# Operand pads, full rows for a filter product, and one wait for two PSUM banks in a hybrid RWKV-7 and Conformer kernel

## The chip, the cores and the metric

The kernel runs on one core of one Trainium2 chip. The metric is the time of one execution on the device in microseconds. A run of this kind gives the same kernel's time within a few tenths of a per cent: the three runs of the kernel before lie between 1447.48 and 1453.27 us, with a median of 1452.06 us. Beside them stands one execution under the hardware profiler, from which all traces here are taken.

## What is computed

A backbone of two layers over 512 latent tokens of 1024 channels, with 256 context tokens as a prefix. Each layer norms its input, scales and shifts it by values made from a conditioning vector, mixes, norms again and adds the result through a gate. All numbers are float32.

```python
def even_mixer(h, hc, ...):            # layer 0
    r, k, v, za, bg, cg, xb, zb = jnp.split(h @ w_in, EVEN_SPLITS, axis=-1)
    # context first: its final states S_f, S_b start the latent scans
    ya, _, _ = rwkv_seq(rwkv_prep(h, r, k, v, *rw), S_f, S_b, r_k, lnx_w, lnx_b, True)
    yb = bg * dwconv(cg * xb, sc_w, seg_len)
    y = jnp.concatenate([ya * silu(za), yb * silu(zb)], axis=-1) @ w_out

def odd_mixer(h, ...):                 # layer 1
    u, gl, z = jnp.split(h @ w_in, 3, axis=-1)        # 1024 -> 3 x 2048
    a = u * jax.nn.sigmoid(gl)
    a = dwconv(a, dw_w, seg_len) + dw_b               # 31 taps in rows of 64 tokens
    a = layer_norm(a, ln_w, ln_b)
    return (silu(a) * silu(z)) @ w_out                # 2048 -> 1024
```

`rwkv_seq` is a recurrence over the tokens, forwards and backwards, with a 64x64 state for each of 16 heads.

## The kernel before, in words

**Dense products.** Every large product is made of float32r matmuls with 128 rows, 128 columns and up to 512 moving elements. To keep float32's precision each operand is split into a high part (cast to float32r) and a low part (what is left), and `mm3` adds three matmuls: high by high, high by low, low by high. `hilo` (lines 119 to 126) loads a weight block, casts it on ScalarE (line 126) and subtracts on VectorE (line 127). All matmuls but the transposes go through line 57, so in the profile they are told apart by their tiles.

**The even layer.** The 16 heads are handled in 8 pairs, the 512 latent tokens in 8 chunks of 64. Within a chunk the recurrence is a triangular system that is solved in one piece, and a short chain passes the state from chunk to chunk. The work comes in 12 stages, 4 for the context (two pairs each) and 8 for the latent tokens (one pair each). In stage s the chain of stage s runs (`chain_lat`: tiles `zol`, `uh`, `UV`, `Hl`, `Ol`), and around it the stages after it are prepared: `solve` (`Xl`, `Yl`, `xtmpl`) and `merge` for s+1, `light` and `heavy` for s+2, and as filling for TensorE the projections and gates (`pl`, `pza`) or a head group of the convolution branch (`conv_branch`: `pcg`, `pxb`, `pbg`, `pzb`).

`heavy` is the part that the change touches. Its function `pa` makes the head products `E` of a pair in four groups (direction z, half g): for two heads h, four products of 64 rows each, written in turn to one PSUM bank for each head (`pal`), then two evictions by VectorE that multiply with a mask (line 601). `pb` transposes the keys of a pair, for each direction 16 transposes in turn into two banks (`pbl`), with two evictions by ScalarE (line 612). Both take their banks from the tag `at`, which has two, and which `light`, `pv`, `po` and others use as well.

**What sets the order.** The kernel is written stage by stage, and a planner that lays out each engine's queue takes, of the instructions that are ready by its own clock, the one written first. It gives the banks of a tag in the order of their first use. `pinned()` (line 561) ties the matmuls of a group to the order in which they are written, but lets other work stand between them. `issue_after` and the `HEAVY_AFTER` table hold a group behind a step of the running chain. On the chip each engine then runs its queue in order, with semaphores between engines.

**The odd layer.** The output product of layer 0 (`o`) and the norm of layer 1 lead to the tiles `h1h` and `h1l`. For each of 4 column blocks n and 4 row blocks m, `products` makes two products `pu` of 24 matmuls each (weights `wc`, in the tags `wa` and `wb`), `gated` joins them and splits the result into `ah`, and the 31-tap convolution is done as a product with a transform of 119 rows (`forward`, tile `px`), a multiplication with the transformed filter, and a product back (`back`, tile `pc`). The tile `ah` holds for each half of 64 tokens the high part in one half of the rows and the low part in the other. `forward` multiplies it with `dfh`, which holds the high part of the transform in both halves (128 rows), and then with `dfl`, the transform's low part, on the 64 rows of the high part alone. Then follow 16 products `pz` of 24 matmuls for z (weights `wz`), and the output product `f` of 384 matmuls (inputs `y`, in the tags `wb` and `xr`; weights `wf`, in the tag `wz`).

**Where tiles lie.** A pool lays its tags one behind the other in SBUF, each rounded up to 32 bytes a partition. In the pool of the odd layer come first `h1h`, `h1l`, `wz`, `a` (all sizes multiples of 64 bytes, starting on one), then `dfc` (960 bytes), `dbe` (32), `dinv` (256), four small ones, and then `pt`, `raw`, `wa` and `wb`: these last ones, `xr` and `pr` start 32 bytes past a multiple of 64. In the even layer the pools of the latent inputs and weights (`hlh`, `hll`, `w`) and of the output product start 32 bytes past one, and so does all that follows the 4-byte tile `ones` up to `xtmp`, the tile `E` among it; `AR`, `BK`, `BKt`, `UV` and `H` start on a multiple.

Of the kernel before, what the change touches and what calls it, by code (L numbers as in the profile page):

```python
# [8 lines left out]
F32 = mybir.dt.float32  # L9
# [42 lines left out]
def kernel(ctx: ExitStack, tc: tile.TileContext, I: dict, out: bass.AP):  # L52
# [14 lines left out]
    def const(name, shape, dt=F32):  # L67
        return cp.tile(shape, dt, tag=name, name=name)

    ident = const("ident", [P, P])  # L70
    epsr = const("epsr", [P, 3])
    G.memset(epsr[:, 0:1], RMS_EPS)
    G.memset(epsr[:, 1:2], LN_EPS)
    G.memset(epsr[:, 2:3], GN_EPS)
    nc.sync.dma_start(ident, I["ident"])

# [90 lines left out]
    def ps_at(name):  # L167
# [8 lines left out]
    SIZE = {"AR": D, "BK": 1536, "BKt": D, "UV": 2 * D, "O": 768, "X": D, "E": 4 * D, "P": 528, "H": 256, "HP": 256,  # L176
            "h0": 256, "PC0": 8, "PC1": 8, "rnq": 48, "xtmp": 136}

# [6 lines left out]
    def small(name, shape):  # L185
        return cvp.tile(shape, F32, tag=name, name=name)

    ones = small("ones", [P, 1])
    G.memset(ones, 1.0)
    omu, hmu, hka, oka = (small(n, [P, k]) for n, k in (("omu", 24), ("hmu", 24), ("hka", 8), ("oka", 8)))  # L190
# [9 lines left out]
    lorl = [[cvp.tile([P, SEQ], F32R, tag=f"{t}{z}", name=f"{t}{z}") for z in range(2)] for t in ("tanhl", "xal")]  # L200
    hlat = tuple(hlp.tile([P, KT, SEQ], F32R, tag=t, name=t) for t in ("hlh", "hll"))
    E0 = w("E", "hctx", F32R).rearrange("p (a k c) -> p a k c", a=2, k=KT)
    hch, hcl = E0[:, 0], E0[:, 1]
# [302 lines left out]
    def lightz(st, z):  # L506
        lat, nm, parts, low, kk = (st[x] for x in ("lat", "nm", "parts", "low", "kk"))
        k_, r_, bon = st["k"], st.get("r"), st.get("bon")
        pl = low(0, z, f"lw{nm}{z}")
        for p, cs in parts:  # L510
            S.activation(sg[:, cs.start // CH : cs.stop // CH, 1:65], ch3(pl[:, cs]), AF.Tanh,
                         bias=hc("w0", z * 8 + p), scale=0.5)
        S.activation(sg[:, :, 1:65], sg[:, :, 1:65], AF.Identity, bias=ones)
        pl = low(1, z, f"la{nm}{z}")
        a = w("a", f"a{nm}{z}")
        for p, cs in parts:
            S.activation(a[:, cs], pl[:, cs], AF.Tanh, bias=hc("a0", z * 8 + p), scale=0.5)
        cumf = w("P", f"P{nm}{z}")
# [41 lines left out]

    def pinned():
        prev = []

        def go(o, lhsT, rhs, start=True, stop=True, op=mm):
            e = op(o, lhsT, rhs, start, stop)
            if prev:
                tc.add_manual_dep(e.ins, prev[-1].name,
                                  mybir.DependencyInfo(mybir.DependencyClass.NoSync, mybir.DependencyReason.DATA),
                                  reason="written order")
            prev[:] = [e.ins]  # L570
            return e

        return go
# [7 lines left out]
    def heavy(st, an=None):  # L581
# [7 lines left out]
        def pa():  # L589
            for gi, (z, g) in enumerate(PA_ORDER if lat else ((0, 0), (1, 0))):  # L590
                with anchored(an, ha[gi if lat else 2 * gi]):
                    AR, BK = st["AR"][z], st["BK"][z]
                    m, x = (4, P) if lat else (8, CH)
                    c0 = m * g
                    pas = [ch3(ps_at(f"pa{nm}{z}{g}{h}"), x) for h in range(2)]
                    go = pinned()
                    for c in range(m):
                        for h in (1, 0):
                            go(pas[h][:, c, :], kb(BK, h, c0 + c), AR[ZR[h], c0 + c, 0:x])
                    for h in range(2):  # L600
                        V.tensor_tensor(out=E[:, h, z * NLAT + c0 : z * NLAT + c0 + m, :], in0=pas[h],  # L601
                                        in1=maskE[:, z * (1 + h) : z * (1 + h) + 1, 0:x].to_broadcast([P, m, x]), op=ALU.mult)

        def pb():
            for z in range(2):
                pbs = [ch3(ps_at(f"pb{nm}{z}{h}")) for h in range(2)]
                go = pinned()
                for c in range(NLAT):
                    for h in (1, 0):
                        go(pbs[h][:, c, :], kb(st["BK"][z], h, c), ident[ZR[h], ZR[h]], op=tr)  # L610
                for h in range(2):
                    S.copy(st["BKt"][z][:, :, ZR[h]], pbs[h])

# [375 lines left out]

    acc0 = outproj(0, ("mm0", "mm1", "at", "at"), ORDER, held, early)  # L990
    l0.close()
    with ExitStack() as l1:
# [71 lines left out]
        dfw = lt("a", "dfw")[:, :NPROD]  # L1064
        dfc = big("dfc", [P, 2 * NPROD + 2], F32R)
        dfh, dfl = dfc[:, :NPROD], dfc[:, NPROD : 2 * NPROD]
        dbe = big("dbe", [P, 8])[:NPROD, 0:1]
        dinv = big("dinv", [NPROD, 64])
# [16 lines left out]
        def dft_stages(n, m, ahl):  # L1085
            pr = [lt("pr", f"pr{n}{m}{s}") for s in range(2)]

            def forward():
# [3 lines left out]
                for s in range(2):  # L1092
                    tp(px[s][:NPROD], dfl[64 * s : 64 * s + 64, :], ahl[s][64 * s : 64 * s + 64, :], False, True)
                for s in range(2):
# [107 lines left out]
        w2 = I["od_w_out"][0]  # L1202
        gg = gate_rows(1)
        xres = [lt("wa", f"xo{m}") for m in range(4)]
        for m in range(4):
# [120 lines left out]
```

## Time and profile before

| | before |
|---|---|
| runs | 1453.27, 1447.48, 1452.06 us |
| median | 1452.06 us |
| the profiled execution | 1451.59 us |
| its span, first to last instruction | 1449.6 us |
| mean granted TensorE clock | 0.979 |

The span is a little shorter than the time of the execution, which has a start and an end around it. In the rows below PE stands for TensorE's matmuls, PEld for its weight loads, DVE for VectorE, ACT for ScalarE, POOL for GpSimd. A row of the timeline gives start, length, engine, line, operation, what is written and read (buffer numbers left out) and how many alike follow each other; matmuls overlap, so their pace is read from start to start, not from their length.

### The profile page before, as it was taken

To read this page: it belongs to the slowest core of one execution; us is meant where nothing else is said; L and a number is where in the kernel's file an instruction comes from. 1 tells how busy PE (TensorE), PEld (TensorE's weight loads), DVE (VectorE), ACT (ScalarE), POOL (GpSimd) and SP (SyncE) were. 2 spreads that over 40 slices of the span, in tenths; PEclk is the share of its full clock that TensorE was granted. 3 is DMA by queue.
4 is the path that set the end of the run, shared out by engine and by line. 5 is a ranking of instruction groups with operands and counts; after the bars stand their busy time and mean duration, and the time that the engine had idled before them with its cause. 6 is when DMAs were issued, how large, how long until landed. Compare 5 with 4: busy or idle time off the path is not lost. (4 is left out here: it accounts for less than half of the span.)

```text
span 1449.6 us, 29729 instructions
## 1 busy us (share of the span) xinstructions
PE 1407.2 (97%) x11921; PEld 1012.7 (70%) x11921; DVE 983.7 (68%) x2294; ACT 749.5 (52%) x1516; POOL 118.2 (8%) x246
## 2 busy tenths in 40 slices
PE   6999999999998999999999999999999999999998
PEld 1564677878776766666676666778777777788876
DVE  2675597568688989999999998557745544544333
ACT  4536364364664665756666565456753323464222
POOL 2023210000101101011011100010000000000000
PEclk9999999979897999999999999999999999999999
DMA  9755433312222321222222212359803303133322
GB/s 324 221 172 160 153 110 98 97 52 71 83 85 74 92 69 59 81 86 60 76 67 83 91 49 84 131 175 324 252 34 102 117 22 95 58 102 91 99 89 86
DMA packets 137626, 158.54 MB, mean 109 GB/s; under 512 B 15375, under 2 KB 104143, under 8 KB 137369
## 3 DMA queue, kind: packets, MB, share of 16 engines
q1 hardware_dynamic: 121104, 106.47, 23.6%
q0 software_dynamic: 15312, 48.99, 10.5%
q8 instruction: 94, 1.54, 0.4%
q10 hardware_dynamic: 1072, 1.19, 0.2%
q14 instruction: 44, 0.36, 0.1%
HBM read 138.33 MB, written 18.28 MB: 108 GB/s over the span
## 5 line engine op out<-in xcount | busy, mean ns | idle before, releaser
L57 PE MATMUL o<-wh,y 128*128 128x512 f32 x248 | 79.7, 397 | 0.0
L658 DVE TENSOR_TENSOR Yl<-Yl,xtmpl 128x126 f32<-128x126 f32 (+22 forms) x248 | 62.2, 251 | 2.7
L656 DVE TENSOR_TENSOR xtmpl<-Xl,Yl 128x126 f32<-128x126 f32 (+22 forms) x248 | 62.0, 250 | 2.7
L57 PE MATMUL pal<-ARl,BKl 64*128 64x128 f32 x512 | 57.8, 306 | 5.5 <-DVE xtmpc L656 2.8
L57 PEld LDWEIGHTS pal<-ARl,BKl 64*128 64x128 f32 x512 | 42.9, 195 | 24.9 <-issue 6.0
L1140 ACT CAST ah<-a 64x512 fp32r<-64x512 f32 x32 | 19.8, 619 | 75.6 <-DVE a L1135 75.2
L57 PE MATMUL zol<-UV,E 64*64 64x64 f32 (+1 forms) x1024 | 54.0, 221 | 0.2 <-ACT UV L764 0.2
L57 PEld LDWEIGHTS o<-wh,y 128*128 128x128 f32 x248 | 45.9, 188 | 9.5
L764 ACT COPY UV<-uh 64x128 f32<-64x128 f32 x128 | 33.3, 260 | 33.5 <-PE uh L57 25.9
L57 PE MATMUL o<-wl,y 128*128 128x512 f32 x124 | 49.4, 398 | 1.2 <-DVE wl L127 1.2
L57 PE MATMUL zol<-Hl,ARl 64*64 64x64 f32 x896 | 50.2, 230 | 0.3
L57 PEld LDWEIGHTS zol<-Hl,ARl 64*64 64x64 f32 x896 | 35.0, 133 | 20.3 <-issue 16.7
L127 DVE TENSOR_TENSOR wl<-wr,wh 128x1024 fp32r<-128x1024 f32 x28 | 34.2, 1223 | 19.6 <-ACT wh L126 19.1
L1135 DVE TENSOR_TENSOR a<-pu,a 128x512 f32<-128x512 f32 x16 | 11.0, 690 | 53.0 <-PE pu L57 50.7
L57 PEld LDWEIGHTS uh<-UV,BKt 128*64 128x64 f32 x704 | 26.7, 138 | 28.5 <-ACT UV L764 23.1
L601 DVE TENSOR_TENSOR E<-pal,maskE 128x512 f32<-128x512 f32 x64 | 43.0, 685 | 3.4 <-PE pal L57 3.0
L57 PEld LDWEIGHTS zol<-UV,E 64*64 64x64 f32 (+1 forms) x1024 | 42.3, 136 | 2.5 <-ACT UV L764 2.0
L1095 DVE SCALAR_TENSOR_TENSOR pr<-px,dbe,What 119x512 f32<-119x512 f32 x32 | 22.6, 745 | 31.1 <-PE px L57 31.1
L126 ACT CAST wh<-wr 128x1024 fp32r<-128x1024 f32 x28 | 29.6, 1056 | 20.7 <-PE o L57 10.4
L771 DVE SCALAR_TENSOR_TENSOR Hl<-uh,PCl,HPl 128x64 f32<-128x64 f32 x112 | 26.4, 277 | 20.1 <-PE uh L57 9.6
L875 POOL DMA_DIRECT2D mwr<-in_mod_w_dram x56 | 29.9, 538 | 114.2 <-PE uh L57 67.4
L57 PE MATMUL uh<-UV,BKt 128*64 128x64 f32 x704 | 36.7, 234 | 2.2 <-ACT UV L764 2.2
(947 smaller groups left out, 4250.9 us busy)
## 6 DMA issues: line engine op xcount, KB each, us to landing
mwr<-in_mod_w_dram POOLq DMA_DIRECT2D x56, 256.0 KB, 3.6
wr<-in_ev_w_out_dram SPq DMA_DIRECT2D x28, 512.0 KB, 5.6
ectx<-in_mod_w_dram SPq DMA_DIRECT2D x12, 512.0 KB, 5.2
wrk<-in_ev_w_in_dram SPq DMA_DIRECT2D x16, 256.0 KB, 3.1
wrv<-in_ev_w_in_dram SPq DMA_DIRECT2D x16, 256.0 KB, 4.6
wrr<-in_ev_w_in_dram SPq DMA_DIRECT2D x16, 256.0 KB, 2.9
wrza<-in_ev_w_in_dram SPq DMA_DIRECT2D x16, 256.0 KB, 2.8
wrcg<-in_ev_w_in_dram SPq DMA_DIRECT2D x16, 256.0 KB, 2.8
```

The lines of the kernel that those rows point to most:

```text
L57: return T.matmul(o, lhsT, rhs, start=start, stop=stop)
L126: S.copy(hi, raw)
L127: env["lo"].tensor_tensor(out=lo, in0=raw, in1=hi, op=ALU.subtract)
L601: V.tensor_tensor(out=E[:, h, z * NLAT + c0 : z * NLAT + c0 + m, :], in0=pas[h], in1=maskE[:, z * (1 + h) : z * (1 + h) + 1, 0:x].to_broad ...
L656: V.tensor_tensor(out=tv, in0=X[:, :i, i : i + 1].to_broadcast([P, i, m]), in1=Y[:, i : i + 1, c0:].to_broadcast([P, i, m]), op=ALU.mult)
L658: V.tensor_tensor(out=Y[:, :i, c0:], in0=Y[:, :i, c0:], in1=tv, op=ALU.add)
L764: u_ = S.copy(UV[ZR[1 - h], i : 2 * nch - i : 2 * nch - 1 - 2 * i, ZR[h]], uh[ZR[1 - h], 0:2, :])
L771: h_ = V.scalar_tensor_tensor(out=Hn[:, z, :], in0=uh[:, 2 + z, :], scalar=PC[z][:, i : i + 1], in1=HP[:, z, :], op0=ALU.mult, op1=ALU.add)
L875: nc.gpsimd.dma_start(mws[q], I["mod_w"][layer, kt * P : (kt + 1) * P, c0 : c0 + 512])
L1095: V.scalar_tensor_tensor(out=pr[s][:NPROD], in0=px[s][:NPROD], scalar=dbe[:, 0:1], in1=What[:, n * 512 : n * 512 + 512], op0=ALU.add, op1= ...
L1135: V.tensor_tensor(out=a, in0=pp[1], in1=a, op=ALU.mult)
L1140: S.copy(ahl[s][hr], a[hr])
```

## The change

Three things change; what is computed stays the same but for a product of two low parts, which `forward` now adds.

1. Pads. `ones` moves from a tile of its own into a fourth column of `epsr`, `xtmp` grows from 136 to 144 words, three tiles of 32 bytes are added to the right-hand pools (`padh`, `pado`, `padq`), and two tiles grow (`dfc` to 1024 bytes, `dbe` to 128). All tiles named above that started 32 bytes past a multiple of 64 start on one, and those that started on one still do.
2. `forward` multiplies `dfl` with all 128 rows of `ah`, as it does with `dfh`.
3. `pinned` takes a list of instructions, and the first matmul of a group waits for all of them. For latent groups these are the evictions of the group before: in `pa` the two masked multiplications of the previous group (for the first group the evictions of `lightz`), in `pb` the last two of `pa` and then the two copies of the first direction.

```diff
-    epsr = const("epsr", [P, 3])
+    epsr = const("epsr", [P, 4])
...
+    ones = epsr[:, 3:4]
+    G.memset(ones, 1.0)
...
-            "h0": 256, "PC0": 8, "PC1": 8, "rnq": 48, "xtmp": 136}
+            "h0": 256, "PC0": 8, "PC1": 8, "rnq": 48, "xtmp": 144}
...
-    ones = small("ones", [P, 1])
-    G.memset(ones, 1.0)
...
+    hlp.tile([P, 8], F32, tag="pad", name="padh")
...
+        st["ev"] = []
         for p, cs in parts:
-            S.activation(sg[:, cs.start // CH : cs.stop // CH, 1:65], ch3(pl[:, cs]), AF.Tanh,
-                         bias=hc("w0", z * 8 + p), scale=0.5)
+            e_ = S.activation(sg[:, cs.start // CH : cs.stop // CH, 1:65], ch3(pl[:, cs]), AF.Tanh,
+                              bias=hc("w0", z * 8 + p), scale=0.5)
+            st["ev"].append(e_)
...
-            S.activation(a[:, cs], pl[:, cs], AF.Tanh, bias=hc("a0", z * 8 + p), scale=0.5)
+            st["ev"].append(S.activation(a[:, cs], pl[:, cs], AF.Tanh, bias=hc("a0", z * 8 + p), scale=0.5))
...
-    def pinned():
+    def pinned(behind=()):
         prev = []
 
         def go(o, lhsT, rhs, start=True, stop=True, op=mm):
             e = op(o, lhsT, rhs, start, stop)
+            if not prev:
+                for x in behind:
+                    tc.add_manual_dep(e.ins, x.ins.name,
+                                      mybir.DependencyInfo(mybir.DependencyClass.Sync, mybir.DependencyReason.DATA),
+                                      reason="both banks free")
...
-                    go = pinned()
+                    go = pinned(st["ev"] if lat else ())
+                    st["ev"] = []
...
-                        V.tensor_tensor(out=E[:, h, z * NLAT + c0 : z * NLAT + c0 + m, :], in0=pas[h],
-                                        in1=maskE[:, z * (1 + h) : z * (1 + h) + 1, 0:x].to_broadcast([P, m, x]), op=ALU.mult)
+                        st["ev"].append(V.tensor_tensor(
+                            out=E[:, h, z * NLAT + c0 : z * NLAT + c0 + m, :], in0=pas[h],
+                            in1=maskE[:, z * (1 + h) : z * (1 + h) + 1, 0:x].to_broadcast([P, m, x]), op=ALU.mult))
...
-                go = pinned()
+                go = pinned(st["ev"] if lat else ())
+                st["ev"] = []
...
-                    S.copy(st["BKt"][z][:, :, ZR[h]], pbs[h])
+                    st["ev"].append(S.copy(st["BKt"][z][:, :, ZR[h]], pbs[h]))
...
+    op.tile([P, 8], F32, tag="pad", name="pado")
...
-        dfc = big("dfc", [P, 2 * NPROD + 2], F32R)
+        dfc = big("dfc", [P, 256], F32R)
...
-        dbe = big("dbe", [P, 8])[:NPROD, 0:1]
+        dbe = big("dbe", [NPROD, 32])[:, 0:1]
...
-                    tp(px[s][:NPROD], dfl[64 * s : 64 * s + 64, :], ahl[s][64 * s : 64 * s + 64, :], False, True)
+                    tp(px[s][:NPROD], dfl, ahl[s], False, True)
...
+        lq.tile([P, 8], F32, tag="pad", name="padq")
```

## The prediction

> **What bounds the kernel now.** I read the page first, then the chain that ended last, then the stretches stage by stage, then single instructions in the timeline.
>
> ```profile
> PE 1407.2 (97%) x11921; PEld 1012.7 (70%) x11921; DVE 983.7 (68%) x2294; ACT 749.5 (52%) x1516; POOL 118.2 (8%) x246
> PEclk9999999979897999999999999999999999999999
> ```
>
> TensorE (PE) is busy 97% of the span of 1449.6 us, and some slices between the eighth and the fourteenth show a lower granted clock. The chain says in which long stretches PE alone decides; its columns are start, length, what, count.
>
> ```profile
> 968.54 31.52 PE o L57 x138
> 1066.79 5.79 PE pu L57 x24
> 1284.61 68.94 PE pz L57 x304
> 1353.56 90.10 PE f L57 x384
> ```
>
> From 1034 us to 1444 us this chain holds hardly anything but matmuls: in the odd layer a nanosecond off a matmul is a nanosecond off the time. The same four rows give paces for one and the same shape (128 rows, 128 columns, 512 wide): o 31.52/138 = 0.2284 us, pz 68.94/304 = 0.2268 us, f 90.10/384 = 0.2346 us.
>
> The latent part of the even layer runs in stages, one a head pair. I cut five of them at the starts of the same matmul group:
>
> ```profile
> 565.00:624.30 59.30, 56.73 (x769) 39.43 (x769) 55.34 (x167) 37.74 (x89) 6.06 (x12) 1.00 0.25 73
> 624.30:682.30 58.00, 57.09 (x769) 39.44 (x769) 54.19 (x162) 37.48 (x89) 6.45 (x13) 1.00 0.26 76
> 682.30:740.90 58.60, 58.06 (x771) 39.70 (x770) 54.03 (x158) 37.15 (x90) 7.76 (x14) 1.00 0.26 76
> 740.90:800.50 59.60, 58.66 (x777) 40.72 (x776) 54.91 (x160) 38.32 (x90) 7.20 (x14) 1.00 0.27 78
> 800.50:859.20 58.70, 57.66 (x773) 39.33 (x772) 53.59 (x156) 37.68 (x91) 3.44 (x7) 1.00 0.22 67
> ```
>
> After the length stand PE, PEld, DVE, ACT, POOL. PE is busy all but 0.5 to 2.6 us of a stage, but VectorE (DVE) is close behind: it idles 3.96, 3.81, 4.57, 4.69 and 5.11 us, 4.4 us in the mean. Here two engines hold the time almost equally, and freeing one meets the other soon.
>
> **Part 1, the pads.** Tile starts, counted up from the sizes and taken modulo 64 bytes: o has both operands 32 past a multiple, pz (from its third weight block on) has both on a multiple, f has its stationary operand (y, in wb and xr) 32 past and its moving one (wf, in wz) on a multiple. Equal offsets run at 0.2284 and 0.2268, unequal at 0.2346. The products pu are unequal too (h1h, h1l on a multiple, the weights in wa and wb 32 past), and the timeline of one gives their pace:
>
> ```profile
> 1125.42 0.40 PE L57 MATMUL pu<-wc116h,h1l 128*128 128x512 f32 x1
> ...
> 1126.12 0.39 PE L57 MATMUL pu<-wc116h,h1l 128*128 128x512 f32 x1
> 1126.35 1.04 PE L57 MATMUL px<-ah,dfc 128*119 128x512 f32 x4
> 1127.32 0.50 PE L57 MATMUL pu<-wc100h,h1h 128*128 128x512 f32 x1
> 1127.66 0.40 PE L57 MATMUL pu<-wc100l,h1h 128*128 128x512 f32 x1
> ```
>
> Three matmuls start to start take 1126.12 - 1125.42 = 0.70 us, 0.2333 each. After the change all of them start on multiples of 64, so I give them the pace of pz, which has the same offsets on both sides already:
> - pu: 4 column blocks x 4 row blocks x 2 halves x 24 = 768 matmuls x (0.2333 - 0.2268) = 5.0 us;
> - f: 384 x (0.2346 - 0.2268) = 3.0 us.
>
> No queue but PE's ends a wait here, so all 8.0 us count. The projections, o and the context products had equal offsets and keep them: nothing. The small products of the state chain read E, which goes from 32 past to a multiple, beside UV:
>
> ```profile
> L57 PE MATMUL zol<-UV,E 64*64 64x64 f32 (+1 forms) x1024 | 54.0, 221 | 0.2 <-ACT UV L764 0.2
> L57 PE MATMUL zol<-Hl,ARl 64*64 64x64 f32 x896 | 50.2, 230 | 0.3
> ```
>
> Those with unequal offsets take 221 ns, those with both on a multiple 230 ns: no sign of a price, so nothing for them. Moving `ones` into `epsr` takes no instruction away; its memset stays on POOL, 8% busy.
>
> **Part 2, the forward filter product with full rows.** The row at 1126.35 holds four matmuls: two of 128 rows, then two of 64 rows that run side by side. From its start to the second pu matmul it is 1127.66 - 1126.35 = 1.31 us for what would be five steps of a stream (px, px, px, px, pu): 5 x 0.2268 = 1.13. The excess is the change to half rows and back, not work. With all four on full rows two matmuls that ran together run one after the other, and both changes go. `dfl` starts 476 bytes into `dfc`, 28 past a multiple of 64, so I leave the two matmuls on it at the slow pace: 1.15 us. Saved: 0.16 x 16 = 2.6 us. By the Trainium skill (page "TensorEngine Tiling (Array Packing)", section "When to Use Tiling") the half rows should have been the better form: a contraction of 64 is to be tiled twofold, for up to double the rate. By that rule alone the change would cost one more matmul in each of 16 places, 16 x 0.23 = 3.7 us; the row above, with the changes of form in it, speaks against it here, and the same page's "Key Properties" says that a change of tiling mode drains the array.
>
> Parts 1 and 2: 10.6 us.
>
> **Part 3, the wait for both banks.** One latent group as it runs now, matmuls and then DVE:
>
> ```profile
> 627.25 0.40 PE L57 MATMUL pbg<-hll,whbg 128*128 128x512 f32 x1
> 627.58 0.48 PE L57 MATMUL pal<-ARl,BKl 64*128 64x128 f32 x2
> 627.99 0.50 PE L57 MATMUL pbg<-hlh,wlbg 128*128 128x512 f32 x1
> 628.33 0.40 PE L57 MATMUL pbg<-hlh,whbg 128*128 128x512 f32 x1
> 628.66 1.16 PE L57 MATMUL pal<-ARl,BKl 64*128 64x128 f32 x14
> 629.74 0.50 PE L57 MATMUL pbg<-hll,whbg 128*128 128x512 f32 x1
> ```
>
> ```profile
> 626.36 0.69 DVE L601 TENSOR_TENSOR E<-pal,maskE 128x512 f32<-128x512 f32 x1 [0.33 <-PE pal L57]
> 627.11 0.68 DVE L601 TENSOR_TENSOR E<-pal,maskE 128x512 f32<-128x512 f32 x1
> ```
>
> The first head product (x2: an f32 matmul leaves two records) starts when the first bank is evicted (626.36 + 0.69 = 627.05) and before the second is (627.11 + 0.68 = 627.79). Then PE is given dense matmuls until the second bank is free, and only then the other fourteen records. The lone product costs: 627.58 - 627.25 = 0.33 instead of 0.23 ahead of it (0.10), itself 0.41, and 628.33 - 627.99 = 0.34 instead of 0.23 behind it (0.11): 0.62 us. Put in front of its fourteen fellows it is nearly free, since they now run in pairs with one left over, and take 629.74 - 628.66 = 1.08. So it goes where the first product waits for the second eviction too; the group ends no later, since the rest waited for that anyway. A key transpose:
>
> ```profile
> 633.21 0.40 PE L57 MATMUL pbg<-hlh,wlbg 128*128 128x512 f32 x1
> 633.60 0.27 PE L576 MATMUL pbl<-ident,BKl 64*128 64x64 f32 x1
> 633.80 0.49 PE L57 MATMUL pbg<-hlh,whbg 128*128 128x512 f32 x1
> ```
>
> It costs 0.20 itself and, by the same two sides, 0.21: 0.41 us. In the timeline 23 of the 32 product groups and 14 of the 16 transposes begin with a lone one; the first and last of each kind:
>
> ```profile
> 438.04 0.46 PE L57 MATMUL pal<-ARl,BKl 64*128 64x128 f32 x2 [0.44 <-DVE BKl L555]
> 868.92 0.49 PE L57 MATMUL pal<-ARl,BKl 64*128 64x128 f32 x2
> 464.49 0.37 PE L576 MATMUL pbl<-ident,BKl 64*128 64x64 f32 x1
> 877.22 0.27 PE L576 MATMUL pbl<-ident,BKl 64*128 64x64 f32 x1
> ```
>
> 23 x 0.62 + 14 x 0.41 = 14.3 + 5.7 = 20.0 us of PE time, or some 2.7 us a stage. Behind the wait on PE stand dense matmuls that could run; they are ahead of the group in the new order, as they are ahead of its rest today. For the first group of a pair the added waits are for ScalarE's evictions, long past; they cost nothing.
>
> Not all of the 20 us reach the end, because DVE is late next. It has 4.4 us of idle time a stage, and what of it ends on PE is small (us, times, longest, for the five stages):
>
> ```profile
> DVE Ol L784 <- PE zol L57: 5.0, 5, 1.4
> DVE Hl L771 <- PE uh L57: 4.8, 10, 0.7
> DVE E L601 <- PE pal L57: 1.7, 6, 0.5
> ```
>
> 11.5 us in five stages, 2.3 a stage, 18 in eight: more than this a shorter PE queue can't give while DVE's work stays. Part of each such wait is the matmul's own way to its result and stays. Bounds: nothing (PE waits for evictions instead), and 18. No row gives the share; I take 7, a third of the 20 and under half of the 18, nearer to nothing because DVE is busy 93% of a stage.
>
> **Sum.** The profiled execution took 1451.59 us, its span 1449.6. 1451.59 - 8.0 - 2.6 - 7 = 1434.0; the median of the runs shown, 1452.06, lies 0.5 above that execution, so I forecast **1434.5 us**.
>
> **Rivals.** *DVE takes it all back*: part 3 gives nothing, PE waits at the evictions for what it saved. For it: 53.59 to 55.34 us of DVE a stage; against it: 4.4 us of idle time. 1452.06 - 10.6 = 1441.5.
>
> *The offsets aren't the cause*: f and pu differ from pz in other ways (which operand is a weight), and the 0.2346 stays. Against it: o has f's roles and runs at 0.2284. 1452.06 - 2.6 - 7 = 1442.5. The Trainium skill ("SBUF — State Buffer", "Operand start alignment") asks only for multiples of the element size and says that its runs timed nothing, so it knows no such price.
>
> *All of it counts*: part 3 gives 18, 1452.06 - 10.6 - 18 = 1423.5.
>
> *Half clock, the slower side*: waiting for both banks leaves PE empty at places where it now has one product, and an empty PE loses its clock:
>
> ```profile
> 437.00:447.00 10.00, 6.58 (x38) 4.53 (x38) 10.00 (x21) 4.96 (x9) 1.98 (x4) 1.00 0.37 102
> 447.00:468.00 21.00, 20.34 (x239) 15.05 (x241) 15.23 (x26) 8.26 (x15) 1.63 (x3) 0.52 0.24 77
> ```
>
> Around the first latent group PE was empty 3.4 of 10 us, and the next 21 us ran at 0.52: 20.34 us of PE work that needs 10 at full clock. One more such stretch costs 10 us, two turn the gain into a loss: 1434.5 + 20 = 1454.5. Against it: in the five stages PE idles 2.6 us at most and keeps 1.00. The Trainium skill ("TensorE: Matmul & The Clock Gate", "A second HAM failure mode: psum-queue depth-cycling") describes this for groups that cycle through PSUM banks.
>
> **How the numbers follow.** About 0.5% (7 us) is what a measurement of this kernel can tell from no change. Chances: the forecast 0.57, DVE takes it back 0.15, the offsets aren't the cause 0.10, all of it 0.10, half clock 0.08. The bound for faster is 1444.8. The forecast, the all-counts case and the DVE case lie below it, the offsets case mostly; one extra half-clock stretch ends at 1444.5, on the bound, two end above 1452. That gives faster 0.86, same 0.09, slower 0.05. The range reaches from 1419 (18 for part 3 and half of a present half-clock stretch gone) to 1446 (the offsets case with some loss, or one stretch more).
>
> **What would show it.** Right: f near 87 us for 384 matmuls and a pu product near 5.64 us; four full-row px and no 64*119 form, with px to the second pu matmul near 1.15 us; pal in runs of 16 records and pbl in runs of 16; stages of 57 to 58 us in which DVE's busy share rises to 95%; the chain unchanged in kind. Wrong: f still at 90; lone pal records left, since then the order was set by something else than the second bank; PE rows that wait on `E` or `BKt` for more than 1 us a stage; a slice with lower PEclk behind 500 us. A half-clock stretch won or lost would move the time by 10 us either way and overrule the rest.

## The result, and the profile after

| | before | after |
|---|---|---|
| median | 1451.3 us (4 runs, 1447.48 to 1453.27) | 1436.8 us (4 runs, 1434.60 to 1437.49) |
| profiled execution, its span | 1451.59, 1449.6 us | 1434.60, 1432.5 us |
| mean granted TensorE clock | 0.979 | 0.982 |

The ratio is 0.9903, with a 95% interval of 0.9888 to 0.9917: 14.1 us less (12.0 to 16.3). The forecast was 1434.5 us, 17.6 less than the median of 1452.06 us known then, with a range of 1419 to 1446. Sign and rough size came as predicted; some terms of the sum did not.

The page of the changed kernel: busy time by engine, and the granted clock in 40 slices.

```profile
PE 1376.7 (96%) x11921; PEld 1008.3 (70%) x11921; DVE 983.0 (69%) x2294; ACT 749.5 (52%) x1516; POOL 117.9 (8%) x246
PEclk9999999979898999999999999999999999999999
```

The same number of instructions keeps TensorE busy 30.5 us less (1407.2 before), and VectorE as long as it did. Of the 30.5 us some 17 reached the span. A part of both numbers is chance: within the span the profiled execution of before spent 58.0 us at half TensorE clock and that of the changed kernel 47.8, and, as the experiments show, the length of such stretches differs between executions of one program. The chain of waits shows what the odd layer did with its part:

```profile
1057.57 5.71 PE pu L57 x24
1064.20 5.46 PE pu L57 x24
1070.68 5.71 PE pu L57 x24
...
1269.93 68.95 PE pz L57 x304
1338.88 80.19 PE f L57 x351
```

`pz`, whose tiles lay right before, has kept its pace (68.94 then). `f` has gone from 90.10/384 = 0.2346 us a matmul to 80.19/351 = 0.2285. One turn over a row block, two `pu` blocks with a filter product behind each, takes 1070.68 - 1057.57 = 13.11 us. The filter product forwards, in the timeline:

```profile
1115.54 1.08 PE L57 MATMUL px<-ah,dfc 128*119 128x512 f32 x4
1116.46 0.39 PE L57 MATMUL pu<-wc100h,h1h 128*128 128x512 f32 x1
1116.69 0.40 PE L57 MATMUL pu<-wc100l,h1h 128*128 128x512 f32 x1
```

Four matmuls of full rows, and 1116.69 - 1115.54 = 1.15 us to the second `pu`, as predicted. The head products and key transposes of the latent stages:

```profile
619.89 1.16 PE L57 MATMUL pal<-ARl,BKl 64*128 64x128 f32 x16
...
625.86 1.16 PE L57 MATMUL pal<-ARl,BKl 64*128 64x128 f32 x16 [1.24 <-DVE E L610]
...
629.70 0.72 PE L584 MATMUL pbl<-ident,BKl 64*128 64x64 f32 x16 [0.41 <-DVE Yl L669]
```

Of the 32 latent product groups one still begins with a lone product (at 839.94 us; it was 23), of the 16 transposes none (it was 14); the sixteen records of a group take 1.09 us from their start to the next matmul. But the second row waits 1.24 us for an eviction by VectorE. The same five stages as in the prediction:

```profile
560.40:619.90 59.50, 55.00 (x772) 39.02 (x771) 55.81 (x168) 37.79 (x89) 6.52 (x12) 1.00 0.25 73
619.90:677.50 57.60, 54.39 (x767) 38.27 (x766) 53.91 (x164) 36.89 (x89) 7.46 (x14) 1.00 0.24 73
677.50:736.10 58.60, 55.99 (x777) 39.48 (x776) 54.68 (x160) 38.27 (x90) 6.71 (x12) 1.00 0.26 79
736.10:794.60 58.50, 56.53 (x778) 39.98 (x777) 54.53 (x157) 37.55 (x89) 6.72 (x12) 1.00 0.27 81
794.60:852.70 58.10, 56.19 (x773) 39.37 (x772) 53.52 (x157) 38.00 (x90) 3.28 (x6) 1.00 0.21 61
```

The first row starts at the group's first product; the prediction's first row starts at 565.00, 0.55 us behind the same product of before, which the timeline has at 564.45. From there the five stages of before are 294.75 us long with 288.74 us of TensorE. Added up, TensorE's busy time fell from 288.7 to 278.1 us, and the length only from 294.7 to 292.3. VectorE has 272.5 us in them, as before. Most of what TensorE gained it now waits for, VectorE above all. Its own queue between the third pair's first head product and the last pair's, five stages again (waited for: us, times, longest); in the five stages of before the same two waits came to 1.3 and 1.1 us:

```profile
PE pal L57 <- DVE E L610: 3.8, 3, 2.2
PE uh L57 <- DVE aml L676: 2.5, 4, 0.8
```

VectorE's waits on TensorE, 11.5 us in the prediction's rows, are now

```profile
DVE Hl L782 <- PE uh L57: 5.1, 9, 0.8
DVE Ol L795 <- PE zol L57: 4.0, 4, 1.4
DVE E L610 <- PE zol L57: 0.5, 1, 0.5
```

So the traces leave two questions: whether the odd layer's part comes from the starts of the tiles at all, and how the waits earned what the sum gave them when the middle stages show so little of it.

### The profile page after: what moved, and what is told of

Read it like the earlier page. It is cut to its first block, busy times and chain, and to the rows that moved or that the text cites. A ratio compares the mean times of both kernels' runs of the same rounds, so it can differ in the third digit from the quotient of the medians.

```text
span 1432.5 us, 29756 instructions
## 1 busy us (share of the span) xinstructions
PE 1376.7 (96%) x11921; PEld 1008.3 (70%) x11921; DVE 983.0 (69%) x2294; ACT 749.5 (52%) x1516; POOL 117.9 (8%) x246
## 4 chain that ended last, share of the span: by engine, by line
PE 63%; DVE 14%; ACT 5%; issue 2%; DMA 0%; DVEq 0%; ACTq 0%
PE pu L57 12%; PE pz L57 6%; PE f L57 6%; PE o L57 5%; PE uh L57 4%; PE zol L57 4%; PE pcg L57 3%; PE pxb L57 3%; PE pza L57 3%; DVE E L610 2%; PE plk L57 2%; PE zoc L57 2%; PE pzb L57 2%; PE plv L57 1%; PE pac L57 1%
## 5 line engine op out<-in xcount | busy, mean ns | idle before, releaser
L57 PE MATMUL pal<-ARl,BKl 64*128 64x128 f32 x512 | 46.3, 300 | 10.7 <-DVE E L610 4.9
L57 PEld LDWEIGHTS pal<-ARl,BKl 64*128 64x128 f32 x512 | 36.4, 194 | 22.2 <-issue 7.2
L886 POOL DMA_DIRECT2D mwr<-in_mod_w_dram x56 | 29.8, 537 | 112.8 <-PE uh L57 67.7
```

The costliest lines, as they stand in the source:

```text
L57: return T.matmul(o, lhsT, rhs, start=start, stop=stop)
L886: nc.gpsimd.dma_start(mws[q], I["mod_w"][layer, kt * P : (kt + 1) * P, c0 : c0 + 512])
```

## The experiments

The theory to be tested: a dense matmul is slow when the starts of its two operands differ modulo 64 bytes (A in the first expectations), and the added waits shorten the even layer because they free TensorE. The rivals: the even layer gained by the pads; VectorE takes everything back; a start off a multiple of 64 is slow by itself.

| kernel | ratio to before | 95% interval | us against 1451.3 |
|---|---|---|---|
| changed kernel | 0.9903 | 0.9888 to 0.9917 | -14.1 |
| pads alone | 0.9966 | 0.9950 to 0.9982 | -4.9 |
| full rows alone | 0.9993 | 0.9967 to 1.0018 | -1.0 |
| waits alone | 0.9965 | 0.9948 to 0.9983 | -5.1 |
| pads and full rows, no waits | 0.9949 | 0.9930 to 0.9968 | -7.4 |
| changed, all starts 32 past | 0.9911 | 0.9886 to 0.9935 | -12.9 |
| before, projections with unequal starts | 1.0007 | 0.9991 to 1.0024 | +1.0 |
| changed, wait of head products alone | 0.9933 | 0.9913 to 0.9953 | -9.7 |
| no waits, merge's copies on ScalarE | 0.9969 | 0.9947 to 0.9991 | -4.5 |
| changed, merge's copies on ScalarE | 0.9908 | 0.9882 to 0.9934 | -13.4 |
| changed, less VectorE work | 0.9906 | 0.9882 to 0.9930 | -13.6 |
| changed, less TensorE work | 0.9890 | 0.9868 to 0.9913 | -16.0 |
| changed, subtractions on POOL | 1.0222 | 1.0198 to 1.0247 | +32.2 |

The median of before moved between 1450.2 and 1452.3 us from group to group of runs, so kernels are compared by their ratios. Within a group, a run's time goes with its mean granted clock: over the 63 runs of before beside these experiments (clocks 0.973 to 0.986) a fitted line gives 1.05 us less for each 0.001 more. The mean clock of a kernel's runs lies between 0.980 and 0.982 in all rows but four: 0.984 with `merge`'s copies on ScalarE and the waits, 0.977 with less VectorE work, 0.974 with less TensorE work, 0.968 with the subtractions on POOL. What this is worth there is said below, as an estimate by that line.

**Pads alone.** The changed kernel with

```diff
-                    go = pinned(st["ev"] if lat else ())
+                    go = pinned()
...
-                go = pinned(st["ev"] if lat else ())
+                go = pinned()
...
-                    tp(px[s][:NPROD], dfl, ahl[s], False, True)
+                    tp(px[s][:NPROD], dfl[64 * s : 64 * s + 64, :], ahl[s][64 * s : 64 * s + 64, :], False, True)
```

> The pads alone: half rows for the low part of the transform, and no added waits. Theory A (a dense matmul is slow when the starts of its two operands differ modulo 64 bytes, and the pads touch nothing else that matters): the traces before and after put pu, px and pc of the odd layer 5.8 us and f 2.4 us shorter; 2.6 of that by the prediction's count are the full rows, so the pads give about 5.7 us, 1451.3 - 5.7 = 1445.6 us, f near 87.7 us, px to the second pu matmul still near 1.31 us, lone head products still there, and the even layer as long as before. Rival B (the even layer gained its 8.6 us through the starts of E and the latent inputs, not through the waits): 1451.3 - 5.7 - 8.6 = 1437 us, with the starts of the head-product groups as early as in the changed kernel (the last of the five stages ending at 853 rather than 859 us).

```profile
1078.32 5.71 PE pu L57 x24
...
1091.59 5.71 PE pu L57 x24
...
1348.76 87.70 PE f L57 x384
```

1451.3 x 0.9966 = 1446.4 us: theory A. `f` takes 2.40 us less. A turn takes 1091.59 - 1078.32 = 13.27 us, against 13.48 with the old starts (below), so `pu` gives 16 x 0.21 = 3.4. The order of TensorE's and VectorE's instructions is that of before, lone products included, and the stages are as long as before.

**Full rows alone.** One line of before:

```diff
-                    tp(px[s][:NPROD], dfl[64 * s : 64 * s + 64, :], ahl[s][64 * s : 64 * s + 64, :], False, True)
+                    tp(px[s][:NPROD], dfl, ahl[s], False, True)
```

> Full rows for the product with dfl alone, all else as before. Theory A (the change of form costs more than the two matmuls that ran side by side): 0.16 us in each of 16 places, 2.6 us less, 1448.7 us; px to the second pu matmul near 1.15 us instead of 1.31. Rival B (the half rows were the cheaper form, as the Trainium skill has it in the page TensorEngine Tiling (Array Packing), section When to Use Tiling): one matmul of 0.23 us more in 16 places, 3.7 us more, 1455.0 us.

```profile
1065.90 5.79 PE pu L57 x24
1072.61 5.61 PE pu L57 x24
1079.23 5.79 PE pu L57 x24
```

The time can't tell 2.6 us from nothing, but excludes 3.7 us more at its upper end of 1.0018, 2.6 us. The trace can tell: a turn is 1079.23 - 1065.90 = 13.33 us. Without the full rows, in the run with the waits alone, it is

```profile
1063.55 5.79 PE pu L57 x24
1070.22 5.80 PE pu L57 x24
1077.03 5.79 PE pu L57 x24
```

1077.03 - 1063.55 = 13.48. So 16 x 0.15 = 2.4 us, and the half rows were the dearer form. The block of 24 behind the filter product also shows what a change of form leaves behind: 5.80 us after half rows, 5.61 after full ones. The other block, 5.79, follows the product back, which still changes form.

**Waits alone.** The kernel before with `st["ev"]` and `pinned(behind)` as in the diff of the change, and in `pa` and `pb`

```diff
-                    go = pinned()
+                    go = pinned(st["ev"] if lat else ())
...
-                go = pinned()
+                go = pinned(st["ev"] if lat else ())
```

> The waits for both banks alone, with the tiles where they lay before and half rows for dfl. Theory A (the waits are what shortened the even layer): lone head products and transposes gone, 1451.3 - 8 = 1443.3 us, f still near 90.1 us; and if the shorter stretch at half clock behind 446 us is the work of the waits, it is 13.65 us long here too instead of 20.48, which is 3.4 of the 8 us. Rival B (VectorE takes back all that the waits free, and the even layer gained by the starts of its tiles): 1450 to 1452 us, the lone products gone all the same, the stretch still 20.48 us.

5.1 us less (2.5 to 7.5): rival B, that the waits give nothing, falls. Theory A's 8 us lie just outside too, and its part about the stretch at half clock falls; this was 17.07 us long here. How long it is does not hang on the change. Three kernels without the added waits, whose order of instructions in the even layer is one and the same, in the window from 440 to 480 us (behind POOL stands the granted clock); before:

```profile
440.00:480.00 40.00, 36.36 (x444) 26.66 (x442) 31.22 (x72) 20.66 (x44) 3.30 (x6) 0.74 0.25 74
```

pads alone:

```profile
440.00:480.00 40.00, 35.11 (x465) 25.68 (x465) 34.72 (x83) 22.79 (x49) 3.31 (x7) 0.91 0.26 78
```

and pads with full rows, here also from 560 to 590 us:

```profile
440.00:480.00 40.00, 36.80 (x453) 27.10 (x454) 32.73 (x79) 21.14 (x48) 3.29 (x6) 0.79 0.24 76
560.00:590.00 30.00, 27.78 (x362) 19.91 (x361) 29.04 (x78) 16.50 (x29) 4.04 (x7) 1.00 0.34 97
```

0.74, 0.91 and 0.79 are stretches of 20.5, 6.8 and 17.1 us at 0.50. They differ by steps of 3.41 us from one execution to the next; a part of the spread of the times is this. The Trainium skill (page "TensorE: Matmul & The Clock Gate", Part 1) says that the gate looks at a free-running window of about 3.4 us, which does not start anew with the kernel; the steps agree with that length. With the waits alone a stretch appears where none was:

```profile
560.00:590.00 30.00, 27.15 (x344) 20.90 (x343) 28.40 (x76) 16.43 (x28) 3.50 (x6) 0.89 0.33 96
```

6.83 us at half clock, and that pair's stage took 62.2 us, where the changed kernel, with the same order of instructions in the even layer, has 60.9: a price of 1.3 us. Of the four profiles with the wait of the head products and the even layer's work as it was, two have it (this one, and that with the wait of the head products alone, at 568 us) and two not (the changed kernel, and that with all starts 32 past); of the five without the waits none has it. The waits alone don't decide it, though: with the copies of `merge` on ScalarE (below) two stretches of 3.4 us stand behind 500 us without the waits as with them. Nor do the times show a lost clock: the 12 runs with the waits alone have a mean of 0.9810, the 29 of before beside them 0.9812.

**All starts 32 past a multiple.** The changed kernel with

```diff
         lp = l1.enter_context(tc.tile_pool(name="lp", bufs=1, reuse_waits="tile"))
+        lp.tile([P, 8], F32, tag="pad", name="padl")
...
-        lq.tile([P, 8], F32, tag="pad", name="padq")
```

> The changed kernel with one tile of 32 bytes put ahead of the odd layer's pool and the pad of the right-hand pool left out, so that h1h, h1l and all weights of the odd layer, y and wf start 32 bytes past a multiple of 64, both operands of each matmul alike. Theory A (only the difference of the two starts counts): as the changed kernel, 1436.8 us within 1.5, f near 87.7 us. Rival B (a start off a multiple of 64 is slow by itself): pu, pz and f, 1536 matmuls at 0.234 instead of 0.227, some 11 us more, 1448 us, f near 90 us.

```profile
1056.09 5.71 PE pu L57 x24
1062.72 5.46 PE pu L57 x24
...
1337.40 87.72 PE f L57 x384
```

0.9911, and the rows as in the changed kernel: only the difference of the two starts counts. The pads need not reach a multiple of 64; they need to be the same on both sides.

**Unequal starts in the even layer.** The kernel before with one line:

```diff
+    hlp.tile([P, 8], F32, tag="pad", name="padh")
     hlat = tuple(hlp.tile([P, KT, SEQ], F32R, tag=t, name=t) for t in ("hlh", "hll"))
```

> The kernel before with one tile of 32 bytes ahead of hlh and hll in their pool: these stay 32 bytes past a multiple of 64, the weights w of the even layer move onto one. 1536 projection matmuls of 512 and 384 of 256 elements, whose operands had equal starts, have unequal ones; nothing else moves, and the odd layer is as before. Theory A (unequal starts are the price, for any tile): a projection matmul takes about 0.234 instead of 0.227 us, 1536 x 0.0065 = 10 us of TensorE time, of which VectorE hides a part in the latent stages: 5 to 10 us more, 1456 to 1461 us. Rival B (the slow pace of f and pu came from something else that the pads changed): the projections keep 0.227, 1451.3 us.

The pace of a run of `plr` matmuls, first and last row; before, 14 steps in 436.99 - 433.81 = 3.18 us, 0.2271 each:

```profile
433.81 0.39 PE L57 MATMUL plr<-hlh,wlr 128*128 128x512 f32 x1
...
436.99 0.39 PE L57 MATMUL plr<-hll,whr 128*128 128x512 f32 x1
```

with unequal starts 18 steps in 436.83 - 432.63 = 4.20 us, 0.2333 each:

```profile
432.63 0.39 PE L57 MATMUL plr<-hll,whr 128*128 128x512 f32 x1
...
436.83 0.40 PE L57 MATMUL plr<-hll,whr 128*128 128x512 f32 x1
```

Its stages from the third pair's first head product to the last pair's, summed (length, then the engines' busy time):

```profile
sum 296.10, PE 289.89 PEld 199.59 DVE 273.62 ACT 188.26 POOL 34.10; mean PE 57.98 PEld 39.92 DVE 54.72 ACT 37.65 POOL 6.82
```

The price is there at once, in other tiles and another layer: half of theory A holds. The other half, 5 to 10 us more, falls: +1.0 us (-1.3 to +3.5). But this does not show that TensorE has time to spare, for the 1536 x 0.0062 = 9.5 us of matmul time that the measured pace would give were not added. The five stages have 289.89 us of TensorE in 296.1 us of length, and without the slowing, with the same order of instructions, 289.25 in 295.7 (next). From start to next start in the timelines, their 477 recorded projection matmuls take 141.8 us, and 141.5 before. Of these, 260 stand beside a product of another form and take 91.4 us in both kernels; only the 217 that stand between two other projection matmuls get slower, from 50.1 to 50.4 us. Over the whole even layer the 951 of that kind take 225.7 us instead of 221.6, and most of this lies ahead of the first latent group. The price shows where such matmuls stream; where small products alternate with them it doesn't. So this run leaves open whether TensorE's load sets the length of those stages, 97.9% busy as it is.

**What the waits are worth, and which.** The changed kernel without the lists,

```diff
-                    go = pinned(st["ev"] if lat else ())
+                    go = pinned()
...
-                go = pinned(st["ev"] if lat else ())
+                go = pinned()
```

> The changed kernel without the added waits: pads and full rows together. The traces of the two parts alone put their odd layers 5.9 and 2.2 us shorter: 1451.3 - 8.1 = 1443.2 us, and the waits are what lies between this and 1436.8, 6.4 us. Rival (the waits do more only where the tiles lie right): 1440 us or less here.

and with that of `pa` alone:

```diff
-                go = pinned(st["ev"] if lat else ())
+                go = pinned()
```

> The changed kernel with the wait of the head products alone; the key transposes are without it, so that one transpose at a time stands between dense matmuls again. The waits as a whole give 1442.9 - 1436.8 = 6.1 us. Theory A (what they give goes by the TensorE time that they free, 14.3 of 20 us by the prediction's count for the head products): 4.4 us here, 1438.5 us. Rival B (what they give comes from the transposes, whose copies start the rest of the pair): 1442 us.

Without the waits the ratio is 0.9949, with them 0.9903: they are worth 6.7 us, by the two intervals some 3 to 10. `pa` alone stands at 0.9933, 1441.6 us: near rival B's 1442, with theory A's 1438.5 just outside its interval; how the 6.7 divides between products and transposes isn't settled by the times. The traces tell where they fall, by one execution of each. Starts in us:

| | no waits | all waits |
|---|---|---|
| head products of the first pair | 437.6 | 437.4 |
| of the third pair | 548.9 | 546.0 |
| of the last pair | 844.6 | 839.9 |
| first `pu` | 1038.5 | 1031.5 |
| first `f` | 1345.7 | 1338.7 |

2.7 us come in the first two latent stages, 1.8 in the next five, 2.3 in the rest of the even layer, nothing behind it. (The stretch at half clock in the first of them was 17.1 us long without and 13.7 with the waits, so a part of the 2.7 is chance: the five profiles without waits took 109.0 to 112.8 us for these two stages, the shortest where the stretch was 6.8 us, and the changed kernel 108.6.) The sums of the five in the middle without waits

```profile
sum 295.70, PE 289.25 PEld 199.53 DVE 273.57 ACT 188.20 POOL 34.12; mean PE 57.85 PEld 39.91 DVE 54.71 ACT 37.64 POOL 6.82
```

and with them

```profile
sum 293.90, PE 279.27 PEld 196.84 DVE 273.91 ACT 188.87 POOL 34.11; mean PE 55.85 PEld 39.37 DVE 54.78 ACT 37.77 POOL 6.82
```

10.0 us of TensorE's time for 1.8 us of length.

**Is it VectorE that takes it?** Two kernels with `merge`'s copies on ScalarE,

```diff
-                (V.tensor_copy if b else S.copy)(E[rs, 1 - z, :, 32 * b : 32 * b + 32], R1[rs])
+                S.copy(E[rs, 1 - z, :, 32 * b : 32 * b + 32], R1[rs])
...
-            (V.tensor_copy if z else S.copy)(Gs[low[z]], ch3(pg[low[z]], 32))
+            S.copy(Gs[low[z]], ch3(pg[low[z]], 32))
...
-            (V.tensor_copy if z else S.copy)(E[top[z], 1 - z, :, 32:64], ch3(px[top[z]], 32))
+            S.copy(E[top[z], 1 - z, :, 32:64], ch3(px[top[z]], 32))
```

> As the run without waits, and in merge the four copies that VectorE makes (two of E from kdml, one of Pml and one of E from uh; 0.42, 0.42, 0.70 and 0.69 us) are made by ScalarE, so VectorE has 2.2 us less in each stage. Theory A (in the latent stages TensorE and VectorE hold the time almost equally): a gain of some 3 us from VectorE alone, 1440 us. Rival B (TensorE alone decides there): 1443 us.

> The changed kernel with the four copies of merge on ScalarE. Theory A (VectorE took back most of the TensorE time that the waits free in the latent stages, 2.4 us came through of 12 in five stages): with VectorE 2.2 us lighter the waits give 10 us or more against the same kernel without them, 1430 us. Rival B (it isn't VectorE: the freed time went into waits that have nothing to do with its load): the waits give the same 6 us as with the heavier VectorE, and this kernel is at 1436.8.

Without the waits neither forecast of a level came: 0.9969, 1446.8 us, lies above both. With them 0.9908, 1437.9 us, is rival B's level. Neither is better than with the copies on VectorE (0.9949, 0.9903). The waits gave 8.8 us here instead of 6.7, but the intervals are wider than that difference, and the mean clocks, 0.980 without and 0.984 with the waits, make up some 4 us of the 8.8 by the line above. The copies stand in the chain that ends with the next pair's `E`, and there ScalarE makes them one after the other; the kernel lost there what VectorE gained, or VectorE's load doesn't decide. So here are two kernels that leave work out, planned as a like amount on each engine. The one leaves out the last steps of the triangular solve (its result is then not the system's):

```diff
-        for i in range(31, 0, -1):
+        for i in range(31, 0 if not st["lat"] else 8, -1):
```

> The changed kernel without the last 8 of the 31 steps of solve for the latent pairs (16 small VectorE instructions of 0.17 to 0.25 us, about 3.5 us by their durations a stage, some 2.6 by their starts); this leaves a part of the triangular system unsolved. Theory A (each stage has a stretch of some 20 us, from the head products to the merge, that VectorE alone decides without a gap, and a stretch of some 40 us that the chain on TensorE decides): nearly all comes through, 8 x 2.6 to 3.5 = 21 to 28 us, 1409 to 1416 us. Rival B (TensorE's work decides the whole stage): nothing or little, 1432 to 1437 us.

the other a third of the matmuls of two projections, in a branch of `proj` that only `pcg` and `pxb` take:

```diff
-    def proj(wt, o, h):
+    def proj(wt, o, h, lean=False):
...
+            if lean:
+                mm(o, wh[:, ks], h[0][:, kt, :], kt == 0, False)
+                mm(o, wl[:, ks], h[0][:, kt, :], False, kt == KT - 1)
+                continue
...
-            proj(wt, pcg, hlat)
+            proj(wt, pcg, hlat, True)
...
-            proj(wt, pxb, hlat)
+            proj(wt, pxb, hlat, True)
```

> The changed kernel without the low-by-high matmuls of the projections pcg and pxb (16 of a stage's matmuls of 0.23 us, 3.7 us a stage, 29 us in eight), so that these are less exact. Theory A (they lie in the stretch that TensorE decides, where the chain of waits names pcg and pxb): more than half of it comes through, 15 to 29 us, 1408 to 1422 us. Rival B (VectorE decides the whole stage, as the run with slower projections lets one think, whose 6 us did not reach the end): 1434 to 1437 us.

Both of theory A's forecasts failed. The sums of the five stages, less VectorE work first,

```profile
sum 292.10, PE 282.65 PEld 198.29 DVE 266.58 ACT 187.84 POOL 33.68; mean PE 56.53 PEld 39.66 DVE 53.32 ACT 37.57 POOL 6.74
```

then less TensorE work:

```profile
sum 288.80, PE 265.80 PEld 187.82 DVE 270.55 ACT 186.59 POOL 34.24; mean PE 53.16 PEld 37.56 DVE 54.11 ACT 37.32 POOL 6.85
```

and in that kernel the longest wait of TensorE's queue in these stages:

```profile
PE pal L57 <- DVE E L614: 9.2, 8, 2.2
```

VectorE lost 7.3 us of busy time (the forecast had counted 13 to 17) and the stages 1.8; TensorE lost 13.5 and the stages 5.1. Over the whole kernel neither time is told from the changed one. With less of its own work TensorE waits 9.2 us for VectorE's evictions of the head products, against 3.8. Both engines are over 91% busy in both runs.

Two things blur this. The order was laid out anew for each kernel. And each had stretches at half clock between 500 and 860 us that the changed kernel had not: two of 10.2 us with less VectorE work, six of 3.4 to 10.2 us with less TensorE work. This is no small thing: the runs' mean clocks of 0.977 and 0.974, against 0.9815 in the changed kernel, are worth some 5 and 8 us by the line above, so a good part of what the lighter work gave was lost again to the lower clock. Stages at full clock show the rest. The fourth of the five in the changed kernel,

```profile
723.50:781.00 57.50, 55.76 (x774) 39.38 (x772) 53.67 (x156) 37.45 (x89) 6.72 (x12) 1.00 0.24 75
```

and with less TensorE work:

```profile
728.00:783.20 55.20, 50.44 (x754) 35.89 (x752) 52.05 (x155) 36.64 (x90) 6.76 (x12) 1.00 0.24 74
```

5.3 us of TensorE less, 2.3 us of length. With less VectorE work the last four stages are at full clock: 230.7 us with 211.6 of VectorE, against 233.0 with 217.0, which is 2.3 of 5.4. So at full clock about two fifths of what was taken off either engine came through, and neither engine's load alone sets the length.

**The subtractions on POOL.** The eight subtractions a stage of `hilo` for `cg`, `xb`, `bg` and `zb`:

```diff
     def lo_for(nm):
-        env["lo"] = V
+        env["lo"] = G if nm[:2] in ("cg", "xb", "bg", "zb") else V
...
+    env["lo"] = V
```

> The changed kernel with the eight subtractions a stage that make the low parts of the convolution branch's weights on POOL instead of VectorE. Theory A (four of them, 0.60 us each, stand in the stretch that VectorE decides): 8 x 2.4 = 19 us less, 1418 us. Rival B (POOL is so much slower, or holds VectorE up so much, that the weights come late or VectorE's own work gets longer): no gain, 1437 us or more.

Rival B, and by much: 32.2 us slower than before, 46 slower than the changed kernel. Some 14 of these go with the lower clock, 0.968, by the line above. The sum of the five stages:

```profile
sum 322.00, PE 292.16 PEld 204.85 DVE 292.90 ACT 189.41 POOL 90.01; mean PE 58.43 PEld 40.97 DVE 58.58 ACT 37.88 POOL 18.00
```

and groups of instructions in them (busy time, mean ns of one):

```profile
L669 DVE TENSOR_TENSOR Yl<-Yl,xtmpl 128x120 f32<-128x120 f32 (+22 forms) x169 | 54.2, 321 | 3.1
L667 DVE TENSOR_TENSOR xtmpl<-Xl,Yl 128x126 f32<-128x126 f32 (+22 forms) x168 | 50.0, 298 | 2.7
...
L610 DVE TENSOR_TENSOR E<-pal,maskE 128x512 f32<-128x512 f32 x40 | 26.2, 685 | 2.8 <-PE pal L57 2.6
...
L129 POOL TENSOR_TENSOR wlcg<-wrcg,whcg 128x512 fp32r<-128x512 f32 x10 | 13.1, 1311 | 28.4 <-ACT whcg L128 27.8 <-PE pbg L57 0.5
```

VectorE gave away 40 x 0.686 = 27.4 us of work and is 19.0 us busier than in the changed kernel, where the two groups of solve steps have a mean of

```profile
L667 DVE TENSOR_TENSOR xtmpl<-Xl,Yl 128x126 f32<-128x126 f32 (+22 forms) x165 | 41.7, 253 | 1.3
L669 DVE TENSOR_TENSOR Yl<-Yl,xtmpl 128x126 f32<-128x126 f32 (+22 forms) x165 | 41.7, 253 | 1.3
```

The eviction of `pal`, with one operand in PSUM, keeps its 685 ns. The Trainium skill (page "SBUF — State Buffer", section "SBUF: two separate sides") says why: VectorE with two inputs in SBUF and GpSimd share a pair of ports, which either holds alone for a whole instruction. Both rows agree. In the five stages the longer solve steps alone, 169 x 0.068 + 168 x 0.045, make up 19.1 us of the 46.4 by which VectorE's remaining work got longer.

No kernel tried was faster than the changed one by more than its interval.

## Why the prediction came right, point by point

- **Pads, 8.0 us.** The mechanism is shown from both sides: equal starts 32 past a multiple are fast, unequal ones slow in either layer wherever such matmuls stream. The size was 5.8. For `f` the prediction took `pz`'s pace of 0.2268 as the goal; `f` came to 0.2284, which is the pace of `o`, quoted there, with the same roles of the operands: 384 x (0.2346 - 0.2284) = 2.4 instead of 3.0. For `pu` the prediction took 0.2268 for all 24 matmuls of a block. That is so in a block with no change of form ahead (5.46 us, and 5.61 with unequal starts, in the run with full rows alone). Behind a change of form the block goes from 5.79 to 5.71 only, with the product back ahead of it in both kernels: 3.4 instead of 5.0. The small products of the state chain, for which it put nothing, took 221 ns before and after.
- **Full rows, 2.6 us.** 16 x 0.15 = 2.4 by the trace, the 1.15 us to the hundredth. The time alone, -1.0 us, does not tell it from nothing.
- **Waits, 7 us.** 6.7, and that the number fits is in part luck: no row gave the share of 7 in 18, as the prediction says. Right: nearly all lone products went, VectorE is late next, and about a third of the 20 us came through. Right too, as a measure for the stages: VectorE's waits on TensorE, 11.5 us in the five, fell to 9.6, which is near what the stages lost, 1.8 to 2.4 us by the landmark. Wrong: the share, for 7 of 18 would have been 4.5 of 11.5 there (57 to 58 us a stage were forecast, 58.5 came, with VectorE at 272.5/292.3 = 93.2% instead of 95%). Nearly three quarters of the 6.7 us came at the two ends of the latent part by the profiles; the prediction had taken the middle stages' figure for all eight.
- **Rivals.** "VectorE takes it all back" is near what the five middle stages show, where 8.2 of 10.0 us went into waits; over the whole it is excluded. "The offsets aren't the cause" and "all of it counts" are excluded. "Half clock" shows in two of four profiles with the wait, as 6.8 us that cost 1.3; at the prediction's price of 10 us for some 21 it would be 3.3. That fits a stage whose length isn't TensorE's load alone. The line through the runs of before lies between: 0.001 of clock is 2.9 us at half clock in a span of 1450, so 1.05 us for 2.9, or 7.4 for 20.5.

**Still open**: what sets the length of the middle stages, and why the waits gave more at the two ends. At full clock it is neither TensorE's load alone (5.3 us less: 2.3) nor VectorE's alone (5.4 less: 2.3). That the cause is the fixed order with mutual waits is argued from the waits, not shown; an order of another making, with the same work, wasn't tried. Nor is it shown why unequal starts cost a stream of matmuls its pace; no offset but 32 bytes was tried.

## What to carry to other kernels

Where one engine alone holds the chain, as in the odd layer, a pace per instruction can be multiplied out and comes true, if the reference row has the same roles, the same starts and the same neighbours. Where two engines are both over 90% busy, a busy share names no bound: change the load of the suspected engine a little and see whether the end moves, before pricing work taken off it, and check in the trace first that its load did change; a price per instruction found in a stream (0.0062 us here) was not paid where small products alternate with the stream. Compare two stages of a trace, and two kernels' runs, at equal granted clock: stretches at half clock come and go with the same program, and came more often where work was taken off TensorE or VectorE.

## What the runs showed of the hardware

- In a stream of its kind, a float32r matmul of 128x128 by 512 goes every 0.227 us when its moving operand and its weights start alike modulo 64 bytes, and every 0.233 us when one is 32 past and the other not (`f`: 0.2284 and 0.2346); equal at 32 is as good as equal at 0. Beside products of another form no price shows (260 projection matmuls: 91.4 us in both cases).
- Two matmuls on full rows, two on half rows side by side and the changes of form around them took 1.31 us, four on full rows 1.15 (both up to the second `pu`). In the chain a block of 24 behind a change of form takes 5.71 us instead of 5.46.
- Stretches at half clock are multiples of 3.41 us and differ from execution to execution (6.8 to 20.5 us at one place) with the order of instructions unchanged. Over 63 runs of the kernel before, the time falls by 1.05 us for each 0.001 of mean granted clock.
- A subtraction of 128x512 takes POOL 1.29 to 1.67 us against VectorE's 0.69, and makes VectorE's own instructions with two SBUF inputs 18 to 27% longer (253 to 298 and 321 ns).
